# A hybrid decoder block: PSUM handed out by phases, score blocks taken two at a time, and another way to the sums of the MLP's entry

## The chip, the core and the metric

The kernel runs on one NeuronCore of a Trainium2 chip. Its time is the device time of one execution in microseconds (us). Five engines work side by side, each through its own queue in order: TensorE multiplies matrices (PE in the rows; PEld is its weight load), VectorE (DVE) and ScalarE (ACT) work on tiles, GpSimd (POOL) on tiles in SBUF, and SyncE (SP) issues transfers. TensorE writes into PSUM, which has eight banks of 512 fp32 values in each of 128 partitions; VectorE and ScalarE read it out.

## What is computed

The reference, cut to what matters (2048 tokens, width 1024, hidden width 4096, 16 query heads of 64 in 2 groups, window 128):

```python
hn = rmsnorm(x, norm_mix_g); proj = hn @ w_in          # LRU | gate | q | k | v
h = rg_lru(causal_depthwise_conv(x_lru), ...);  y_lru = h * gelu(g_lru)
scores = einsum(q, kwin) * scale                        # blocks of 128 queries, 2 key blocks
m = maximum(max(scores), sink); p = exp(scores - m)
probs = p / (sum(p) + exp(sink - m));  y_attn = einsum(probs, vwin)
x = x + concat(rmsnorm(y_lru), rmsnorm(y_attn)) @ w_out
hm = rmsnorm(x, norm_mlp_g)
x = x + square(relu(hm @ w_mlp_up)) @ w_mlp_down
return rmsnorm(x, norm_final_g)
```

## The kernel before

The tokens are taken in two chunks of 1024. Each chunk goes through input projection, attention, LRU, output projection and the up half of the MLP; the down half follows for both. Every matrix operand is split into a high part (made by ScalarE) and a low part (VectorE, `low = raw - high`), and a product is three matmuls: high by high, high by low, low by high.

**The order.** The program is written in Python as pieces of loops, and a list scheduler puts each engine's instructions into one fixed queue; the semaphore waits come from the tiles that an instruction reads or writes. A tile in PSUM has a tag, and a new tile of a tag waits until the readers of the last one are done. What is tracked is the tile, so two halves of one tile count as one.

**PSUM.** Two tiles of two banks each (tags mm0 and mm1) and four single banks (b01 twice, b2, b3) serve everything up to the end of the MLP's up half.

**Attention.** Heads come in turn (variable s, 16 passes a chunk). A pass has four steps p, and each step has: the scores of head s for two blocks (`scores`, 4 matmuls into a bank of tag b01, line L610), the products with the values of an older step (`values`, 24 short matmuls, L664), the transposes of the probabilities of head s - 1 (`probs`, two, L640, into one half of the bank tpb), and a piece of a projection (`piece`, 6 matmuls into a two-bank tile, L236 to L239; qps is the projection of a later pair of heads). VectorE puts the mask into the scores (L615 to L618), takes the maximum (L620, L621), and writes the low part of the transposed probabilities (pf, L644). When the projection of a pair of heads is complete (every second pass), ScalarE and VectorE read it out for one head and then for the other (L588 high, L589 low, named qs). A low weight tile wlo comes once for such a pair (L179).

**The MLP's up half.** It follows Strassen and Winograd: the normed activations hm are cut into quarters B11, B12, B21, B22, and their sums T1 = B12 - B11, T2 = B22 - T1, T3 = B22 - B12 and T4 = T2 - B21 are made once for a chunk, at its entry. Transposed blocks of the last token tiles arrive in PSUM (tps). VectorE takes T1 (L344) and T2 (L346) from them; ScalarE copies B12 into a tile x3 (L345), and VectorE subtracts it from B22 in PSUM to get T3 (L349). T1 overwrites B11 in the tile braw. The function `sums` then makes T4 (L365) and splits all into high (ScalarE, L360) and low (VectorE, L361). The low part of T2 is L350.

After that, 16 times a chunk, `pair(fp)` makes seven products of 12 matmuls (L410): A11 B11, A12 B21, S2 T2, A22 T4, S3 T3, S1 T1 and S4 B22, with weight sums S1 to S4 that GpSimd prepares (L388 to L391). pa and pb are single banks, and qr is a tile of two banks whose halves are pq (for A22 T4) and pr (for S1 T1, then S4 B22):

```python
qr = mm("qr", fp % 2)
pq, pr = qr[:, :HALF], qr[:, HALF:]
```

L440 reads pq on VectorE (`c2[:, lo] = pq + s3`); L443 reads pr after S1 T1, and L448 reads it after S4 B22. L453 to L456 combine the results. s12h and s12l are the high and low parts of S1 and S2, f2h and f2l those of S3 and A22, a1h and a1l those of A11 and A12.

The functions that the diff touches:

Of the kernel before, what the change touches and what calls it, by code (L numbers as in the profile page):

```python
# [37 lines left out]
def hybrid_block_kernel(  # L38
# [36 lines left out]
    def f32(ap):  # L75
        return ap.bitcast(F32)
# [5 lines left out]
    ps_stack = ExitStack()  # L82
    mmp = ps_stack.enter_context(tc.tile_pool(name="mmp", bufs=1, space=PSUM))
    hbp = ps_stack.enter_context(tc.tile_pool(name="hbp", bufs=1, space=PSUM))
# [26 lines left out]
    def bank(i, name, shape=(P, HALF)):  # L111
        if i < 2:
            return hbp.tile(list(shape), F32, name=name, tag="b01", bufs=2)
        return hbp.tile(list(shape), F32, name=name, tag=f"b{i}")
# [7 lines left out]
    def mm(name, i=None):  # L122

        if i is None:
            i = mm_next[0]
            mm_next[0] ^= 1
        return mmp.tile([P, D], F32, name=name, tag=f"mm{i}")

    def mm_halves(name, i=None):
        ps = mm(name, i)  # L130
        return [ps[:, :HALF], ps[:, HALF:]]
# [167 lines left out]
    class Up:  # L299
# [18 lines left out]
        def token_tile(self, t, src, g):  # L318
# [16 lines left out]
            if t == NT // 2 + 1:  # L335
                two = (P, 2, HALF)
                self.x3 = [U(q, "x3", F32, two) for q in range(2)]
                self.y2 = [U((2, 7)[q], "y2", F32, two) for q in range(2)]
                self.h["T2"] = self.quarter([H_TAG(0, p_, 2 + q) for p_ in range(2) for q in range(2)])
                self.h["B22"] = self.quarter([H_TAG(1, p_, 2 + q) for p_ in range(2) for q in range(2)])  # L340
            for q in range(2):
                o12, o22 = os[q], os[2 + q]
                t1, x3, y2 = self.braw[q][:, :, ts], self.x3[q][:, :, ts], self.y2[q][:, :, ts]
                dve.tensor_tensor(t1, o12, t1, op=ALU.subtract)  # L344
                act.activation(x3, o12, AF.Copy)  # L345
                dve.tensor_tensor(y2, o22, t1, op=ALU.subtract)  # L346
                hq = self.h["T2"]
                act.activation(hq[0][q][:, :, ts], y2, AF.Copy)
                dve.tensor_tensor(x3, o22, x3, op=ALU.subtract)  # L349
                dve.tensor_tensor(hq[1][q][:, :, ts], y2, f32(hq[0][q][:, :, ts]), op=ALU.subtract)  # L350
# [4 lines left out]
        def sums(self):  # L355
# [11 lines left out]
            split("T3", ("u6", "u3", "u5", "u4"), self.x3)  # L367
            split("T1", ("u8", "u9", "u2", "u7"), self.braw[:2])
# [48 lines left out]
        def pair(self, fp):  # L417

            pa, pb = bank(fp % 2 * 2, "pa"), bank(fp % 2 * 2 + 1, "pb")
            qr = mm("qr", fp % 2)  # L420
            pq, pr = qr[:, :HALF], qr[:, HALF:]
# [74 lines left out]
    def new_kv():  # L496
        k = mm("kps", 1)
        return k, ((k[:, :HALF], k[:, HALF:]), pair(0, "vps"))
# [11 lines left out]
    for c in range(NCH):  # L510
# [83 lines left out]
        class Head:  # L594
# [41 lines left out]
            def probs(self, p):  # L636

                tp = tpb[:, p % 2]
# [143 lines left out]
        for s in range(NH + 1):  # L782
            j = s // 2
            if s < NH:
                if s % 2 == 0:
                    yqs[j] = U(3 + j % 2, "yq", F32, (P, NT, P))
                heads[s] = Head(s, qs[j][s % 2], yqs[j])
# [5 lines left out]
            for p in range(4):  # L793
                if s < NH:
                    heads[s].scores(p)
                    if p == 3:
                        heads[s].sums()
# [3 lines left out]
                if s > 0:  # L801
                    heads[s - 1].probs(p)
                    late.append((s - 1, p))
                    if p == 3 and s % 2 == 1 and s > 1:
                        flip(j - 1, yqs[j - 1])
                piece(p if s % 2 else 4 + p)
# [118 lines left out]
        r_lr = token_rstd(accq, "lr")  # L925

# [166 lines left out]
    ps_stack.close()  # L1093
# [185 lines left out]
```

## Time and profile before

| | |
|---|---|
| median of 3 runs | 2512.08 us (2510.38 to 2513.5) |
| the profiled execution | 2512.32 us |
| its span, first to last instruction | 2510.6 us |
| TensorE busy | 2420.6 us (96% of the span) |
| VectorE busy | 1766.3 us (70%) |
| ScalarE busy | 1254.5 us (50%) |
| GpSimd busy | 457.4 us (18%) |
| mean granted TensorE clock | 0.996 of full speed |

The span is the profiled execution between its first and its last instruction, and its own time is 1.7 us more. Matmuls are pipelined, so one that lasts 0.39 us can be followed by the next after 0.23 us, and the busy time is that in which at least one is under way.

### The profile page before, as it was taken

Reading aid. Unit: us, or ns where it says so; the run is one execution under the profiler, and the core shown is the slowest. Engines: PE = TensorE matmul, PEld = TensorE weight load, DVE = VectorE, ACT = ScalarE, POOL = GpSimd, SP = SyncE. Lnnn points to the kernel's source line nnn. Section 1 sums busy time; section 2 is a strip of 40 time slices with the busy share of each in tenths; the row PEclk is TensorE's granted clock in tenths of the full one; section 3 lists DMA queues with packets and bytes.
Section 4 is the critical chain, followed back from the end, with each engine's and each line's share of the span. In section 5 each row is a group of like instructions: output and inputs, shape, how many; then the busy total and the mean of one; then the engine's idle time right before and its main releaser. Section 6 shows DMA issues by size and latency. Waiting matters only on the chain.

```text
span 2510.6 us, 32534 instructions
## 1 busy us (share of the span) xinstructions
PE 2420.6 (96%) x12338; PEld 1974.2 (79%) x12338; DVE 1766.3 (70%) x2400; ACT 1254.5 (50%) x2084; POOL 457.4 (18%) x455
## 2 busy tenths in 40 slices
PE   7999999999999998999999998999999999999998
PEld 6877787787788877887778787788878877888886
DVE  6887566756655565886667847655564898887889
ACT  6666777414455455666778315444554233322335
POOL 0445000001333210454000001322310110111100
PEclk9999999999999999999999999999999999999999
DMA  4111113312344443111113312344464454443334
GB/s 161 37 52 52 45 46 107 115 51 100 118 142 155 157 155 130 43 52 51 46 45 124 111 42 101 133 145 146 148 212 129 154 163 147 142 138 122 125 98 164
DMA packets 132812, 276.37 MB, mean 110 GB/s; under 512 B 11184, under 2 KB 70576, under 8 KB 132656
## 3 DMA queue, kind: packets, MB, share of 16 engines
q1 hardware_dynamic: 124880, 246.50, 29.4%
q0 software_dynamic: 5184, 18.88, 2.0%
q10 hardware_dynamic: 2592, 8.91, 0.9%
q8 instruction: 97, 1.59, 0.3%
q14 instruction: 59, 0.48, 0.1%
HBM read 190.37 MB, written 83.89 MB: 109 GB/s over the span
## 4 chain that ended last, share of the span: by engine, by line
PE 66%; DVE 15%; issue 9%; ACT 7%; DMA 2%; POOL 1%; POOLq 0%; SPq 0%; ACTq 0%; DVEq 0%
PE dd L1187 14%; PE ops L960 10%; PE qr L410 10%; PE pa L410 9%; PE pb L410 3%; PE sc L610 2%; PE qps L239 2%; PE qps L236 2%; PE qps L237 2%; DVE xc L719 2%; DVE acc L1196 1%; PE xps L237 1%; PE xps L236 1%; PE xps L239 1%; DVE wlo L179 1%
## 5 line engine op out<-in xcount | busy, mean ns | idle before, releaser
L1196 DVE TENSOR_TENSOR acc<-dd,acc 128x1024 f32<-128x1024 f32 x211 | 255.4, 1219 | 85.1 <-PE dd L1187 84.6
L960 PE MATMUL ops<-whi,ht 128*128 128x512 f32 x1024 | 278.4, 391 | 1.0 <-DVE x L965 1.0
L990 ACT ACTIVATE ah<-araw 128x1024 fp32r<-128x1024 f32 x96 | 101.9, 1062 | 293.0 <-PE dd L1187 286.6
L960 PEld LDWEIGHTS ops<-whi,ht 128*128 128x128 f32 x1024 | 192.2, 188 | 42.7 <-DVE x L965 2.5
L960 PE MATMUL ops<-wlo,ht 128*128 128x512 f32 x512 | 159.7, 391 | 0.6 <-DVE wlo L179 0.5
L388 POOL TENSOR_TENSOR s<-wraw 128x512 f32<-128x512 f32 x32 | 43.0, 1343 | 593.2 <-issue 321.0
L178 ACT ACTIVATE whi<-wraw 128x1024 fp32r<-128x1024 f32 x84 | 88.5, 1054 | 120.7 <-PE ops L960 86.2
L647 POOL TENSOR_SCALAR_AFFINE_SELECT pf<-pf 128x512 f16<-128x512 f16 x128 | 87.3, 682 | 333.4 <-DVE pf L644 327.0
L991 DVE TENSOR_TENSOR al<-araw,ah 128x1024 fp32r<-128x1024 f32 x96 | 123.4, 1287 | 11.0 <-ACT ah L990 10.9
L624 ACT ACTIVATE st<-sc,mx 128x128 f32<-128x128 f32 x256 | 91.6, 364 | 60.1 <-DVE mx L621 59.6
L179 DVE TENSOR_TENSOR wlo<-wraw,whi 128x1024 fp32r<-128x1024 f32 x84 | 106.5, 1274 | 20.0 <-ACT whi L178 9.5
L960 PEld LDWEIGHTS ops<-wlo,ht 128*128 128x128 f32 x512 | 95.5, 188 | 21.4 <-DVE wlo L179 2.3
L236 PE MATMUL qps<-ht,whi 128*128 128x512 f32 x256 | 107.8, 421 | 0.0
L396 ACT ACTIVATE f2h<-wraw 128x1024 fp32r<-128x1024 f32 x32 | 33.9, 1061 | 142.6 <-DMA act<-hid 111.9
L237 PE MATMUL qps<-ht,whi 128*128 128x512 f32 x256 | 101.7, 397 | 0.0
L236 PE MATMUL xps<-ht,whi 128*128 128x512 f32 x256 | 101.5, 397 | 0.0
L239 PE MATMUL qps<-ht,wlo 128*128 128x512 f32 x256 | 101.3, 396 | 0.0
L237 PE MATMUL xps<-ht,whi 128*128 128x512 f32 x256 | 101.0, 394 | 0.0
L236 PE MATMUL gpps<-ht,whi 128*128 128x512 f32 x256 | 100.8, 394 | 0.0
L410 PE MATMUL qr<-hm,s 128*128 128x512 f32 x384 | 97.6, 403 | 2.7 <-DVE hid L443 2.7
L237 PE MATMUL gpps<-ht,whi 128*128 128x512 f32 x256 | 100.1, 391 | 0.0
L397 DVE TENSOR_TENSOR f2l<-wraw,f2h 128x1024 fp32r<-128x1024 f32 x32 | 39.1, 1223 | 79.1 <-ACT f2h L396 79.1
(327 smaller groups left out, 6852.5 us busy)
## 6 DMA issues: line engine op xcount, KB each, us to landing
araw<-act SPq DMA_DIRECT2D x96, 512.0 KB, 3.5
wraw<-in_w_up_dram SPq DMA_DIRECT2D x64, 512.0 KB, 3.2
act<-hid SPq DMA_DIRECT2D x128, 256.0 KB, 2.6
wraw<-in_w_in_dram SPq DMA_DIRECT2D x52, 512.0 KB, 3.2
act<-a SPq DMA_DIRECT2D x96, 256.0 KB, 2.6
wraw<-in_w_out_dram SPq DMA_DIRECT2D x32, 512.0 KB, 3.2
braw<-in_w_down_dram SPq DMA_DIRECT2D x28, 512.0 KB, 4.3
xt<-in_x_dram SPq DMA_DIRECT2D x16, 512.0 KB, 4.6
```

The lines of the kernel that those rows point to most:

```text
L178: act.activation(hi, raw, AF.Copy)
L179: (eng or dve).tensor_tensor(lo, raw, f32(hi), op=ALU.subtract)
L236: pe.matmul(ps[m], w[0][:, k * P:(k + 1) * P], hk(ht[m][0], k), start=(k == 0), stop=False)
L237: pe.matmul(ps[m], w[0][:, k * P:(k + 1) * P], hk(ht[m][1], k), start=False, stop=False)
L239: pe.matmul(ps[m], w[1][:, k * P:(k + 1) * P], hk(ht[m][0], k), start=False, stop=(k == KT - 1))
L410: pe.matmul(ps, w[a_][:, ks], hk(h[b_], k), start=first and k == 0 and i == 0, stop=k == KT // 2 - 1 and i == 2, skip_group_check=True)
L624: ins = act.activation(self.st[:, b, :], cur[:, i, :], AF.Exp, bias=self.mx[:, b:b + 1], accum_out=self.ls[:, b:b + 1])
L960: pe.matmul(ps[m], a_, wk[k][b_][:, hs], start=(k == 0 and a_ is yh and b_ == 0), stop=(k == kn - 1 and a_ is ylo))
L990: act.activation(hi, raw, AF.Copy)
L991: dve.tensor_tensor(lo, raw, f32(hi), op=ALU.subtract)
L1187: pe.matmul(o[:, i, :], a_[:, t0:t0 + P], b_[:, r, :], start=first and r == 0 and k == 0, stop=r == 1 and k == 2, skip_group_check=True)
L1196: dve.tensor_tensor(accs[blk][d_], o, accs[blk][d_], op=ALU.add)
```

## The change

It has three parts.

First, PSUM is opened anew for each phase. A function `psum` closes the pools of the last phase and opens the next. In the phases "sbp" (the start, the output projection and the MLP's up half) there are eight single banks s0 to s7; in the phase "doubles" (from the keys and values to the end of the LRU) there are the two double tiles and four single banks as before. In the MLP pq and pr thereby become two tiles, and what was qr is gone.

Second, attention takes the steps p two at a time: two score blocks, then the older values, then two sets of transposes, then two pieces. The transposes of odd steps no longer go to tpb, but to halves of the double tile that no projection uses at the time (`free`); even steps keep a half of tpb each.

Third, at the MLP's entry T1 gets a tile of its own (t1) and no longer overwrites B11 in braw. The copy x3 and its subtraction from PSUM are gone; T3 is made in `sums` as T2 - B11 from tiles in SBUF (`t3 = y2 - braw`, which is B22 - B12 again), in one subtraction of 1024 columns for each of the two q.

```diff
     slots = ctx.enter_context(tc.tile_pool(name="slots", bufs=1))
-    ps_stack = ExitStack()
-    mmp = ps_stack.enter_context(tc.tile_pool(name="mmp", bufs=1, space=PSUM))
-    hbp = ps_stack.enter_context(tc.tile_pool(name="hbp", bufs=1, space=PSUM))
+    phase = [None, {}]
+    def psum(*names):
+        if phase[0]:
+            phase[0].close()
+        phase[:] = [ExitStack(), {}]
+        for name in names:
+            phase[1][name] = phase[0].enter_context(
+                tc.tile_pool(name=name, bufs=1, space=PSUM, reuse_waits="tile"))
+    def doubles():
+        psum("mmp", "hbp")
+    psum("sbp")
...
     def bank(i, name, shape=(P, HALF)):
+        if "sbp" in phase[1]:
+            return half(4 + i, name)
         if i < 2:
-            return hbp.tile(list(shape), F32, name=name, tag="b01", bufs=2)
-        return hbp.tile(list(shape), F32, name=name, tag=f"b{i}")
+            return phase[1]["hbp"].tile(list(shape), F32, name=name, tag="b01", bufs=2)
+        return phase[1]["hbp"].tile(list(shape), F32, name=name, tag=f"b{i}")
+    def half(i, name):
+        return phase[1]["sbp"].tile([P, HALF], F32, name=name, tag=f"s{i}")
...
             mm_next[0] ^= 1
-        return mmp.tile([P, D], F32, name=name, tag=f"mm{i}")
+        return phase[1]["mmp"].tile([P, D], F32, name=name, tag=f"mm{i}")
     def mm_halves(name, i=None):
+        if "sbp" in phase[1]:
+            if i is None:
+                i = mm_next[0]
+                mm_next[0] ^= 1
+            return [half(2 * i, name), half(2 * i + 1, name)]
         ps = mm(name, i)
...
                 two = (P, 2, HALF)
-                self.x3 = [U(q, "x3", F32, two) for q in range(2)]
+                self.t1 = [U(q, "t1", F32, two) for q in range(2)]
                 self.y2 = [U((2, 7)[q], "y2", F32, two) for q in range(2)]
                 self.h["T2"] = self.quarter([H_TAG(0, p_, 2 + q) for p_ in range(2) for q in range(2)])
                 self.h["B22"] = self.quarter([H_TAG(1, p_, 2 + q) for p_ in range(2) for q in range(2)])
             for q in range(2):
                 o12, o22 = os[q], os[2 + q]
-                t1, x3, y2 = self.braw[q][:, :, ts], self.x3[q][:, :, ts], self.y2[q][:, :, ts]
-                dve.tensor_tensor(t1, o12, t1, op=ALU.subtract)
-                act.activation(x3, o12, AF.Copy)
+                t1, y2 = self.t1[q][:, :, ts], self.y2[q][:, :, ts]
+                dve.tensor_tensor(t1, o12, self.braw[q][:, :, ts], op=ALU.subtract)
                 dve.tensor_tensor(y2, o22, t1, op=ALU.subtract)
-                hq = self.h["T2"]
-                act.activation(hq[0][q][:, :, ts], y2, AF.Copy)
-                dve.tensor_tensor(x3, o22, x3, op=ALU.subtract)
-                dve.tensor_tensor(hq[1][q][:, :, ts], y2, f32(hq[0][q][:, :, ts]), op=ALU.subtract)
+                act.activation(self.h["T2"][0][q][:, :, ts], y2, AF.Copy)
+            hq = self.h["T2"]
+            for q in range(2):
+                dve.tensor_tensor(hq[1][q][:, :, ts], self.y2[q][:, :, ts], f32(hq[0][q][:, :, ts]),
+                                  op=ALU.subtract)
             hq = self.h["B22"]
...
             split("T4", ("u16", "u17", "u18", "u19"), t4)
-            split("T3", ("u6", "u3", "u5", "u4"), self.x3)
-            split("T1", ("u8", "u9", "u2", "u7"), self.braw[:2])
+            t3 = self.braw[:2]
+            for q in range(2):
+                dve.tensor_tensor(t3[q], self.y2[q], t3[q], op=ALU.subtract)
+            split("T3", ("u6", "u3", "u5", "u4"), t3)
+            split("T1", ("u8", "u9", "u2", "u7"), self.t1)
...
             pa, pb = bank(fp % 2 * 2, "pa"), bank(fp % 2 * 2 + 1, "pb")
-            qr = mm("qr", fp % 2)
-            pq, pr = qr[:, :HALF], qr[:, HALF:]
+            pq, pr = half(fp % 2 * 2, "pq"), half(fp % 2 * 2 + 1, "pr")
             lo, hi = slice(0, HALF), slice(HALF, D)
...
     def new_kv():
+        doubles()
         k = mm("kps", 1)
...
-            def probs(self, p):
-                tp = tpb[:, p % 2]
+            def probs(self, p, free):
+                if p % 2 and free:
+                    tp = free[p // 2][:, :2 * P].rearrange("p (a n) -> p a n", a=2)
+                else:
+                    tp = tpb[:, p // 2]
                 for i in range(2):
...
             j = s // 2
+            free = mm_halves("tp", (s + 1) // 2 % 2) if 0 < s < NH - 1 else None
             if s < NH:
...
                     piece, done = (new_x if j + 2 == KT else new_gate)(0)
-            for p in range(4):
+            for p0 in (0, 2):
                 if s < NH:
-                    heads[s].scores(p)
-                    if p == 3:
+                    for p in (p0, p0 + 1):
+                        heads[s].scores(p)
+                    if p0:
                         heads[s].sums()
                 if len(late) == 4:
                     for _ in range(2):
                         heads[late[0][0]].values(late.pop(0)[1])
                 if s > 0:
-                    heads[s - 1].probs(p)
-                    late.append((s - 1, p))
-                    if p == 3 and s % 2 == 1 and s > 1:
+                    for p in (p0, p0 + 1):
+                        heads[s - 1].probs(p, free)
+                        late.append((s - 1, p))
+                    if p0 and s % 2 == 1 and s > 1:
                         flip(j - 1, yqs[j - 1])
-                piece(p if s % 2 else 4 + p)
+                for p in (p0, p0 + 1):
+                    piece(p if s % 2 else 4 + p)
             if s % 2 == 0:
...
         r_lr = token_rstd(accq, "lr")
+        psum("sbp")
...
     up.run(ahead)
-    ps_stack.close()
+    phase[0].close()
     ddp = ctx.enter_context(tc.tile_pool(name="ddp", bufs=4, space=PSUM, reuse_waits="tile"))
```

Lines of the new kernel are about 22 to 35 higher: L589 is L614, L640 is L668, L644 is L672, L664 is L692, L410 is L435, L440 is L464, L443 is L467, L365 is L387, L361 is L383. T3's subtraction is L391.

What moves in the queues. On VectorE in attention, this stands in a queue of a steady pair of heads from the weight tile wlo to the first pf after the projection's read-out (qs); before:

```order
L179 TENSOR_TENSOR wlo<-wraw,whi 128x1024 [waits DMAHW0_49,PE_49]
L632 TENSOR_TENSOR ls<-ls,es 128x8 [waits Activation_49]
L615 COPY_PREDICATED sc<-prevm,negt 128x128 [waits PE_49]
L633 TENSOR_SCALAR ls<-ls 128x8 [waits DVE_49]
L616 COPY_PREDICATED sc<-prevm,sc 128x128 [waits DVE_49]
L634 RECIPROCAL ls<-ls 128x8 [waits DVE_49]
L620 TENSOR_REDUCE mx<-sc 128x2 [waits DVE_49]
L589 SCALAR_TENSOR_TENSOR qs<-qps,qs 64x1024 [waits Activation_49]
L621 TENSOR_SCALAR mx<-mx,snk 128x2 [waits DVE_49]
L644 SCALAR_TENSOR_TENSOR pf<-tp,pf 128x256 [waits Activation_49]
```

and now:

```order
L201 TENSOR_TENSOR wlo<-wraw,whi 128x1024 [waits DMAHW1_49,PE_49]
L640 COPY_PREDICATED sc<-prevm,negt 128x128 [waits PE_49]
L614 SCALAR_TENSOR_TENSOR qs<-qps,qs 64x1024 [waits Activation_49]
L641 COPY_PREDICATED sc<-prevm,sc 128x128 [waits DVE_49]
L643 COPY_PREDICATED sc<-prevm,sc 128x2x128 [waits PE_49]
L645 TENSOR_REDUCE mx<-sc 128x2 [waits DVE_49] x2
L614 SCALAR_TENSOR_TENSOR qs<-qps,qs 64x1024 [waits Activation_49]
L646 TENSOR_SCALAR mx<-mx,snk 128x2 [waits DVE_49] x2
L672 SCALAR_TENSOR_TENSOR pf<-tp,pf 128x256 [waits PE_49,Pool_49]
```

The small row sums ls (L632 to L634) stand ahead of wlo now; both score blocks of the double step (three copies and two maxima) stand between the first qs and the second.

On TensorE the same pair of heads has two groups of 12 projection matmuls in a pass in place of four groups of 6. Over both chunks, places where transposes into tp are followed by another kind of work go from 116 to 100, and for all transposes from 167 to 149. The first transposes of an odd step into the free tile, in the pass that follows the read-out, stand behind the scores of a double step, 24 values, two transposes, 12 projection matmuls and 8 more values, and wait for VectorE and TensorE.

On TensorE in the MLP, this stands where S1 T1 begins (s12h) in a steady pair; before:

```order
L410 MATMUL pa<-hm,a1l 128x512
L410 MATMUL pb<-hm,a1h 128x512
L410 MATMUL qr<-hm,s12h 128x512 [waits DVE_49]
L410 MATMUL qr<-hm,s12h 128x512
L410 MATMUL qr<-hm,s12l 128x512
```

and now:

```order
L435 MATMUL pa<-hm,f2h 128x512 x2
L435 MATMUL pa<-hm,f2l 128x512
L435 MATMUL pr<-hm,s12h 128x512 x2
L435 MATMUL pr<-hm,s12l 128x512
L435 MATMUL pr<-hm,s12h 128x512 x2
```

S1 T1 stands behind S3 T3 (f2h, f2l into pa) and has no wait for VectorE any more; before, it stood behind A11 B11 and the first matmul of A12 B21 of the next pair. S4 B22 keeps its wait for VectorE (L467), with four matmuls of the next pair ahead of it.

On VectorE at the first chunk's entry into the MLP, for the last token tile (y is T2, t is T1, hm the split parts of all sums); before:

```order
L344 TENSOR_TENSOR braw<-tps,braw 128x2x256 [waits PE_49]
L344 TENSOR_TENSOR braw<-tps,braw 128x2x256 [waits Activation_49]
L346 TENSOR_TENSOR y_5816<-tps,braw 128x2x256 [waits DVE_49,PE_49]
L349 TENSOR_TENSOR x_5814<-tps,x_5814 128x2x256
L346 TENSOR_TENSOR y_5817<-tps,braw 128x2x256 [waits DVE_49]
L349 TENSOR_TENSOR x_5815<-tps,x_5815 128x2x256 [waits Activation_49]
L350 TENSOR_TENSOR hm<-y_5816,hm 128x2x256 [waits Activation_49]
L350 TENSOR_TENSOR hm<-y_5817,hm 128x2x256 [waits Activation_49]
L365 TENSOR_TENSOR braw<-braw,y_5816 128x1024
L224 TENSOR_TENSOR hm<-tps,hm 128x2x256 [waits Activation_49]
L365 TENSOR_TENSOR braw<-braw,y_5817 128x1024
```

and now:

```order
L366 TENSOR_TENSOR t_5865<-tps,braw 128x2x256 [waits PE_49]
L366 TENSOR_TENSOR t_5866<-tps,braw 128x2x256 [waits PE_49]
L367 TENSOR_TENSOR y_5867<-tps,t_5865 128x2x256 [waits DVE_49,PE_49]
L367 TENSOR_TENSOR y_5868<-tps,t_5866 128x2x256 [waits DVE_49,PE_49]
L387 TENSOR_TENSOR braw<-braw,y_5867 128x1024 [waits DVE_49]
L371 TENSOR_TENSOR hm<-y_5867,hm 128x2x256 [waits Activation_49]
L371 TENSOR_TENSOR hm<-y_5868,hm 128x2x256 [waits Activation_49]
L246 TENSOR_TENSOR hm<-tps,hm 128x2x256 [waits Activation_49] x2
L387 TENSOR_TENSOR braw<-braw,y_5868 128x1024
L383 TENSOR_TENSOR hm<-braw,hm 128x1024 [waits Activation_49]
L391 TENSOR_TENSOR braw<-y_5867,braw 128x1024
```

The two x rows and ScalarE's copies in front of them are gone, T1 and T2 follow one another, the first T4 subtraction stands ahead of T2's low part, and the T3 subtraction (L391, two in all) stands between the low parts of T4. Up to the low part a1l, the queue has 20 rows from the first T1 row before and 18 now. On TensorE 75 MLP matmuls stand ahead of the first that needs a1l, where 66 stood; and ScalarE's s12h for the second pair now waits for the last matmul of the first pair's S1 T1, which stands right ahead of the second pair's S2 T2.

## Rows read from the trace of the kernel before

**Rows 1.** The page, part 1: busy time, share of the span, instructions.
```profile
PE 2420.6 (96%) x12338; PEld 1974.2 (79%) x12338; DVE 1766.3 (70%) x2400; ACT 1254.5 (50%) x2084; POOL 457.4 (18%) x455
```

**Rows 2.** TensorE's waits: total us, times, longest.
```profile
PE tp L640 <- DVE pf L644: 13.2, 16, 1.1
...
PE pa L410 <- ACT hm L348: 7.1, 2, 3.5
...
PE qr L410 <- DVE hid L440: 5.5, 4, 4.2
```

**Rows 3.** Busy time by stretch, attention and MLP: us, PE, PEld, DVE.
```profile
50.00:250.00 200.00, 190.54 (x1675) 159.72 (x1675) 161.26 (x417) 124.17 (x398) 91.41 (x135) 1.00 0.13 46
650.00:930.00 280.00, 279.38 (x1208) 224.21 (x1207) 155.43 (x175) 139.18 (x165) 82.40 (x56) 1.00 0.43 147
```

**Rows 4.** Timeline of TensorE in attention: start, us, what.
```profile
118.16 0.44 PE L640 MATMUL tp<-ident,st 128*128 128x128 f32 x2 [0.83 <-DVE pf L644]
...
125.33 0.40 PE L610 MATMUL sc<-kcar,qs 128*128 128x256 f32 x2
...
125.80 0.87 PE L664 MATMUL av<-vpa,pf 128*128 128x64 f16 x24
126.51 0.42 PE L640 MATMUL tp<-ident,st 128*128 128x128 f32 x2
126.69 0.48 PE L236 MATMUL qps<-ht,whi 128*128 128x512 f32 x1
127.00 0.40 PE L237 MATMUL qps<-ht,whi 128*128 128x512 f32 x1
```

**Rows 5.** Timeline of VectorE in attention, same pair of heads.
```profile
113.14 1.63 DVE L179 TENSOR_TENSOR wlo<-wraw,whi 128x1024 fp32r<-128x1024 f32 x1
...
116.30 1.22 DVE L589 SCALAR_TENSOR_TENSOR qs<-qps,qs 64x1024 fp32r<-64x1024 f32 x1
...
117.69 0.42 DVE L644 SCALAR_TENSOR_TENSOR pf<-tp,pf 128x256 f16<-128x256 f32 x1
...
118.93 1.23 DVE L589 SCALAR_TENSOR_TENSOR qs<-qps,qs 64x1024 fp32r<-64x1024 f32 x1
```

**Rows 6.** Timeline of TensorE in one steady MLP pair.
```profile
783.92 0.39 PE L410 MATMUL pb<-hm,a1h 128*128 128x512 f32 x1
784.20 0.73 PE L410 MATMUL qr<-hm,s12h 128*128 128x512 f32 x2
784.77 0.39 PE L410 MATMUL qr<-hm,s12l 128*128 128x512 f32 x1
...
787.05 0.39 PE L410 MATMUL pb<-hm,a1h 128*128 128x512 f32 x1
```

**Rows 7.** Timeline of VectorE in the same pair.
```profile
783.46 0.68 DVE L440 TENSOR_TENSOR hid<-qr,s 128x512 f32<-128x512 f32 x1
```

**Rows 8.** Timeline of VectorE at the first chunk's MLP entry.
```profile
627.58 0.69 DVE L344 TENSOR_TENSOR braw<-tps,braw 128x512 f32<-128x512 f32 x1 [0.66 <-ACT x L345]
...
633.52 1.71 DVE L365 TENSOR_TENSOR braw<-braw,y 128x1024 f32<-128x1024 f32 x1
...
644.76 1.21 DVE L378 TENSOR_TENSOR a1l<-wraw,a1h 128x1024 fp32r<-128x1024 f32 x1
```

**Rows 9.** Timeline of TensorE at that entry.
```profile
630.50 0.51 PE L410 MATMUL pa<-hm,s12h 128*128 128x512 f32 x1 [3.54 <-ACT hm L348]
...
646.03 0.50 PE L410 MATMUL pa<-hm,a1l 128*128 128x512 f32 x1
```

**Rows 10.** Timeline of GpSimd at that entry.
```profile
634.23 2.17 POOL L389 TENSOR_TENSOR s<-s,wraw 128x512 f32<-128x512 f32 x1
```

**Rows 11.** Timeline of TensorE at the second chunk's MLP end.
```profile
1870.24 1.19 PE L410 MATMUL qr<-hm,s12h 128*128 128x512 f32 x2 [4.18 <-DVE hid L440]
...
1875.64 3.06 PE L410 MATMUL qr<-hm,s 128*128 128x512 f32 x12 [0.79 <-DVE hid L443]
```

**Rows 12.** Timeline of VectorE there.
```profile
1869.51 0.68 DVE L440 TENSOR_TENSOR hid<-qr,s 128x512 f32<-128x512 f32 x1
```

## Prediction

> **What bounds the kernel now.** I read the page's busy times first: TensorE is busy 2420.6 us of a span of 2510.6, so at most 90 us can be had without taking matmuls away, and the change takes none away [rows 1]. The waits of TensorE come second, since only what ends one of them counts: the longest sum is 13.2 us in 16 waits of transposes in attention for VectorE's pf, then 7.1 us at the two MLP entries and 5.5 us of S1 T1 for L440, of which one wait alone is 4.2 [rows 2]. The windows come third: TensorE leaves 9.5 of 200 us idle in attention, where VectorE is busy 161 of 200, and 0.6 of 280 in the steady MLP, where VectorE is busy 155 [rows 3]. So VectorE, in order and four fifths full, sets attention's pace at the moments when TensorE needs it, while in the MLP little more than the beat of the matmuls is to be had. Then I followed each place in the timelines.
>
> **Attention.** Once in a pair of heads the second transposes wait 0.83 us, until 118.16 [rows 4]. The cause is VectorE's queue: the weight tile wlo starts at 113.14, the first read-out qs at 116.30 takes 1.22, and only then comes the pf (117.69, 0.42) that has to leave the bank which both transposes share [rows 5]. After the change that wait goes, since odd steps have a tile of their own. But that tile is the one from which qs was read, so the first odd transposes now wait for the second qs read-out. In the old order this ends at 118.93 + 1.23 = 120.16, 7.0 us after wlo's start [rows 5].
>
> I walk the new order from wlo's start (0). VectorE: wlo 1.2 to 1.6 (1.63 at 113.14 [rows 5]), one short mask copy, the first qs to about 2.9, then copies and two maxima, about 1.5 (an estimate from the 0.42 of pf, which is of the same 256 columns), the second qs from 4.2 to 5.4. TensorE, from the projection's last matmul, which I take to fall on the same moment, since the first read-out waits for it: two groups of scores at 0.47 each (125.33 to 125.80), 24 values 0.71 (to 126.51), two transposes 0.18 (to 126.69), and 12 projection matmuls, 0.31 for the first and 0.23 for each of the others [rows 4, 6], 2.8 in all, then 8 values 0.24: the odd transposes are reached at 4.9. The new wait is 0.5 (0.3 to 0.8 with wlo's two durations). The next, even, transposes wait for a pf that stands right behind the second qs, ready at 6.1, when TensorE comes at 5.9 to 6.1: 0 to 0.35. I take 0.65 for a pair; bounds 0.3 and 1.15. For 16 such waits that is 10.4 in place of 13.2: **-2.8** (-8.4 to +5).
>
> A matmul behind transposes starts 0.31 after the one before it, not 0.23 [rows 4, 6]; 18 such places fewer at 0.08 give **-1.4**. The scores, values and transposes themselves stay the same in number.
>
> **The steady MLP.** In a pair S1 T1 starts at 784.20, 0.28 after the matmul before it, where 0.23 is the beat (787.05 - 784.77 over 10 matmuls), and its third matmul follows after 0.57 in place of 0.46: 0.05 + 0.11, so 0.17 lost [rows 6]. It waits for L440, which begins at 783.46, takes 0.68 and reads pq, the other half of the same tile [rows 7]. With two tiles this wait is gone from the order. About 30 of the 32 pairs are steady: **-5.1**. The bound on the other side is 0: S4 B22 still waits for VectorE (L467), now with S1 T1 earlier, and L464 and L467 may stand in one another's way there.
>
> **The MLP's entries.** VectorE is the bound from the last token tile's transposes to a1l: its first T1 waits 0.66 us at 627.58 for ScalarE's copy, and a1l ends at 644.76 + 1.21 = 645.97 [rows 8]; TensorE waits 3.54 for T2 until 630.50, and the first matmul with a1l comes at 646.03 [rows 9]. Out go two subtractions of 512 columns at 0.69 on VectorE and the wait of 0.66; one row of 512 columns for the hidden sum moves behind a1l, 0.69 again; in come two subtractions of 1024 columns at 1.21: 2.7 less and 2.4 more, so a1l ends within 0.3 of where it did. T2's high part no longer stands behind two copies on ScalarE and comes 0.5 to 1 earlier. What counts then is that 75 matmuls stand ahead of the first with a1l, not 66: 9 x 0.23 = 2.0, and with the 0.5 at the start 2.5. Against it stands s12h for the second pair, which now waits for the last S1 T1 of the first, right ahead of that pair's S2 T2: a read-out of 1.1 to 1.2 us (I take a ScalarE tile of 1024 columns to last as VectorE's 1.21 [rows 8]) that nothing covers. **-1.3** for a chunk, **-2.6** for both; bounds -6 and 0.
>
> The same subtraction L365 took 1.71 us at 633.52, while GpSimd was at 634.23 in an addition of weights [rows 8, 10], and 1.21 is what a1l of the same size takes without GpSimd. So the two new subtractions can cost 0.5 more each where they meet GpSimd, 1.0 for a chunk. The Trainium skill (SBUF — State Buffer, Who interferes with whom) says that a VectorE instruction with two inputs in SBUF and a GpSimd instruction that reads SBUF shut each other out of a shared port, while one with a single SBUF input does not; by that rule the change trades two subtractions that GpSimd can't delay for two that it can, which speaks against it. The longer row agrees in its direction, and by the rule the entries would give -0.6 in place of -2.6.
>
> **The end of the second chunk's MLP.** S1 T1 waits 4.18 us until 1870.24 [rows 11] for L440, which VectorE reaches only at 1869.51, behind tiles of the down half [rows 12]. It does not need L440's result, only the release of pq's half. Afterwards it can run in that gap, at once behind S3 T3, and S4 B22 waits for L467 instead. It started at 1875.64 [rows 11]. L467 still stands in the same queue behind the same down-half tiles, and by that queue ends near 1872.4 to 1873.9. So **-2.5** (-1.7 to -3.2). The same mechanism is smaller at the first chunk's end, where the transposes of the next chunk fill in; I count nothing there, with 2 to either side.
>
> **The sum.** -2.8 - 1.4 - 5.1 - 2.6 - 2.5 = -14.4 from the profiled execution's 2512.3, whose span is 2510.6 and which lies 0.2 above the median of the three runs: about 2498. A measurement of this kernel tells 0.2% (5 us) from no change.
>
> **Rivals.**
> - *The second qs is late (slower).* If VectorE stays as far behind as in the old order, where that read-out ends 7.0 after wlo, the odd transposes wait 2.0 us for a pair, not 0.83: 16 x 1.2 = +19, and with the other terms (-11.6) +7: 2519. For it: VectorE is 81% busy, and whatever delays its queue by 1 us hits TensorE at once, for the two transposes in the shared tile have no cover. Against it: the two qs come closer together in the new order, without the row sums and the pf that stood between. It outweighs the rest once the wait exceeds about 1.6 us in each pair.
> - *Gains given back at the next wait (no change).* Attention at its bad bound (+5 - 1.4), S4 B22 taking over the 0.17 in each steady pair, the entries at 0, and only the tail's -2.5: +1: 2513. For it: in each place the instruction behind the removed wait waits for the same engine. Against it: in the steady MLP VectorE is busy only 155 of 280 us [rows 3].
> - *The new wait in attention is at its short bound (faster still).* -8.4 - 1.4 - 5.1 - 4 - 3.2 = -22: 2490. It needs VectorE to finish the second qs before 4.9.
> - *The entry does nothing.* VectorE's queue there is as long as before. Then the sum is -12 and the case is still the main one, at 2500.
>
> **The numbers.** The main case 0.58 (2492 to 2505, 2498 the likeliest), the short bound 0.12, given back 0.18, the late qs 0.12. The range leaves out the latter's upper part and the lower half of the third: 2487 to 2515. Faster by over 0.2%: 0.58 + 0.12 = 0.70; within: 0.18; slower: 0.12.
>
> **What would show it.** In attention the wait of transposes for pf (13.2) shrinks, and one for the qs read-out comes up, under 0.8 us each; over 1.6 makes me wrong. In the steady MLP the first of S1 T1's matmuls follows at the beat, and a pair takes 0.17 less; if S4 B22's wait grows by as much, that term is 0. At the entry TensorE meets T2 before 630 and a1l about where it did. At the second chunk's end no wait above 2 us stands before S1 T1, and the first matmul of the down half comes 1.7 to 3.2 sooner.

## The result and the profile after

The changed kernel takes 2569.7 us (2564.96 to 2572.04), the kernel before 2511.2 beside it: a ratio of 1.023 (1.0211 to 1.025). It is 58 us slower where I forecast 14 faster. From the page of the changed kernel (span, then busy time, share of the span and instructions):

```profile
span 2570.3 us, 32626 instructions
...
PE 2433.8 (95%) x12338; PEld 1991.5 (77%) x12338; DVE 1741.4 (68%) x2396; ACT 1251.3 (49%) x2076; POOL 447.7 (17%) x455
```

It has the same 12338 matmuls, and no engine has more instructions than before [rows 1]. VectorE, ScalarE and GpSimd are a little less busy. TensorE is busy 13.2 us longer with the same matmuls; the mean granted clock fell from 0.996 to 0.979 of full speed, and I put the 13.2 down to that. So of the 59.7 us that the span grew, 46.5 are waiting and 13.2 slower matmuls, and nothing is new work. TensorE's waits after the change (total us, times, longest):

```profile
PE sqt L729 <- POOL accq L935: 44.2, 2, 22.6
...
PE tp L668 <- DVE qs L614: 8.3, 6, 2.5
PE pr L435 <- DVE hid L467: 7.7, 4, 2.2
...
PE tp L668 <- DVE pf L672: 1.4, 3, 0.8
```

The wait of the attention transposes for pf (13.2 before [rows 2]) is nearly gone, and one for the read-out qs stands in its place, as foretold. But 44.2 us go by in two waits that the prediction does not name: sqt, the transposes for the LRU's row sums, wait for GpSimd's last addition into accq, once a chunk. Before the change it is

```profile
PE sqt L701 <- POOL accq L901: 2.7, 2, 1.7
```

so these two waits alone grew by 41.5 us. TensorE at the first of them, in the kernel before:

```profile
459.27 1.09 PE L701 MATMUL sqt<-ident,accq 128*128 128x128 f32 x8 [0.99 <-POOL accq L901]
```

and in the changed one:

```profile
444.05 0.39 PE L915 MATMUL gps<-xhi,gd 128*128 128x512 f32 x1
467.00 1.97 PE L729 MATMUL sqt<-ident,accq 128*128 128x128 f32 x8 [22.56 <-POOL accq L935]
468.62 1.20 PE L995 MATMUL ops<-whi,ht 128*128 128x512 f32 x2
```

Between the LRU's last gate matmuls (gps) and sqt lies the chain of the LRU's last columns: sigmoids, table loads and exponentials on ScalarE, products and a scan on VectorE, the square, and GpSimd's addition. That chain is little shorter in the kernel before: from the last gps matmul to sqt it takes 21.3 us in both chunks there, and 23.0 and 22.3 now. GpSimd's addition alone takes 2.36 and 2.35 us before, 3.69 and 3.49 now. What filled the chain is seen in the windows (us, then busy time and instructions of PE, PEld, DVE, ACT, POOL; PEclk; DMA share and GB/s) of the 23 us ahead of sqt, first in the kernel before:

```profile
436.00:459.00 23.00, 21.95 (x95) 17.33 (x93) 20.32 (x24) 18.79 (x25) 3.75 (x4) 1.00 0.57 196
```

and then in the changed one, in the first chunk, the 13 us behind that gap, and in the second chunk:

```profile
444.00:467.00 23.00, 0.44 (x3) 0.01 (x2) 17.31 (x18) 17.25 (x22) 5.29 (x4) 0.54 0.57 202
467.00:480.00 13.00, 13.00 (x55) 11.02 (x56) 5.82 (x10) 0.37 (x2) 1.12 (x2) 0.89 0.32 110
1403.00:1426.00 23.00, 1.34 (x6) 0.80 (x5) 15.72 (x17) 16.33 (x20) 5.65 (x5) 0.50 0.57 204
```

89 of the 95 matmuls there are of the output projection (ops), on the attention half of its input, which needs nothing of the LRU; the others are the last gps. Now there are 3 or 6 in all, gps and sqt, and no ops. In and right after the gap TensorE has the lower of its two clock levels (0.5 of full speed, 1.2 GHz): the two matmuls at 468.62 take 1.20 us together, and the granted clock of the 13 us from 467 is 0.89.

The order of TensorE's queue says the same: before the change 110 output-projection matmuls of a chunk stand ahead of sqt, 26 of them even ahead of the last gps; after the change none does. `psum("sbp")` stands in the program behind `r_lr = token_rstd(accq, "lr")` and ahead of the loop of the output projection. It closes the pools of which sqt's tiles are the last and opens the one from which every ops tile comes; and in the queue all ops now stand behind all of the old phase's matmuls.

The start times of some instructions in the traces show where it goes; each figure is the changed kernel's start less that of the kernel before, in us, and what is added between two rows is lost there:

| first start of | chunk 0 | chunk 1 |
|---|---|---|
| first scores | +3.4 | +38.3 |
| sqt for accq | +7.7 | +35.2 |
| last matmul of the output projection | +31.7 | +61.6 |
| last matmul of the MLP's up half (S4 B22) | +29.6 | +59.4 |

So 24.0 and 26.4 us are lost in the two output projections, 3.4 at the start, and 8.7 from the first chunk's MLP to the second's scores (38.3 less 29.6). The attention and LRU stretches give +4.3 and -3.1, the MLPs -2.1 and -2.2. The 3.4 at the start, which every run with the phases shows (2.8 to 4.1), I did not trace.

The 8.7 has the same form. TensorE after the first chunk's last product:

```profile
984.56 0.41 PE L240 MATMUL tps<-ident,xt 128*128 128x128 f32 x2 [2.27 <-DVE xt L230]
...
986.92 2.82 PE L240 MATMUL tps<-ident,xt 128*128 128x128 f32 x12 [0.65 <-DVE xt L230]
992.86 0.80 PE L258 MATMUL kps<-ht,whi 128*128 128x512 f32 x1 [3.12 <-DVE ht L246]
```

`new_kv` opens the double phase, and kps is its first tile. It stands behind all transposes (tps) of the next chunk's input, of the old phase; before, 16 of them stood among the kps matmuls, which covered their waits. Behind these waits the clock is low here too:

```profile
992.00:1003.00 11.00, 10.14 (x32) 8.12 (x33) 1.94 (x3) 1.06 (x1) 0.00 (x0) 0.68 0.71 239
```

At a granted clock of 0.68 these 11 us are about 3.5 lost (an estimate, 0.32 x 11), so a good part of the 8.7 is the clock and not the waits.

### The profile page after: what moved, and what is told of

Same layout as the page of the kernel before. It is cut to its first block, busy times and chain, and to the rows that moved or that the text cites. A ratio compares the mean times of both kernels' runs of the same rounds, so it can differ in the third digit from the quotient of the medians.

```text
span 2570.3 us, 32626 instructions
## 1 busy us (share of the span) xinstructions
PE 2433.8 (95%) x12338; PEld 1991.5 (77%) x12338; DVE 1741.4 (68%) x2396; ACT 1251.3 (49%) x2076; POOL 447.7 (17%) x455
## 4 chain that ended last, share of the span: by engine, by line
PE 66%; DVE 16%; issue 8%; ACT 7%; POOL 1%; DMA 1%; POOLq 0%; SPq 0%; ACTq 0%; DVEq 0%
PE dd L1222 14%; PE ops L995 13%; PE pa L435 9%; PE pr L435 7%; PE pq L435 3%; PE pb L435 3%; DVE xc L747 2%; PE sc L635 1%; DVE acc L1231 1%; PE xps L259 1%; PE xps L258 1%; PE xps L261 1%; DVE wlo L201 1%; DVE qs L614 1%; DVE r L926 1%
## 5 line engine op out<-in xcount | busy, mean ns | idle before, releaser
L675 POOL TENSOR_SCALAR_AFFINE_SELECT pf<-pf 128x512 f16<-128x512 f16 x128 | 96.2, 751 | 336.7 <-DVE pf L672 329.1
L1000 DVE SCALAR_TENSOR_TENSOR x<-ops,rs_at,x 128x512 f32<-128x512 f32 x96 | 67.6, 745 | 61.6 <-PE ops L995 56.1
L435 PE MATMUL pr<-hm,s 128*128 128x512 f32 x384 | 101.3, 415 | 7.7 <-DVE hid L467 7.7
```

Of the source, the lines that this page charges most:

```text
L435: pe.matmul(ps, w[a_][:, ks], hk(h[b_], k), start=first and k == 0 and i == 0, stop=k == KT // 2 - 1 and i == 2, skip_group_check=True)
L675: nc.gpsimd.affine_select(out=pf[:, 1], in_=pf[:, 0], compare_op=ALU.is_gt, fill=0.0, base=0, pattern=[[0, 4], [-1, P]], channel_multiplier=1)
```

## The experiments

I took the theory that the switch between pools is what costs (A), and against it that the new work in attention or at the entry makes the gaps (B).

**Keeping the double phase.** The changed kernel without the switch at the output projection and without a second opening of the same phase; pq and pr are halves of one tile again:

```diff
         r_lr = token_rstd(accq, "lr")
-        psum("sbp")
...
     def new_kv():
-        doubles()
+        if "mmp" not in phase[1]:
+            doubles()
...
-            pq, pr = half(fp % 2 * 2, "pq"), half(fp % 2 * 2 + 1, "pr")
+            qr = mm("qr", fp % 2)
+            pq, pr = qr[:, :HALF], qr[:, HALF:]
```

> The changed kernel, but PSUM stays in the double-tile phase from the first keys and values to the end of the MLP's up half: no switch ahead of the output projection, none back at the second chunk, and so pq and pr are halves of one tile again. Attention's double steps and the entry's new sums stay. Theory A: the switch of pools puts the 110 output-projection matmuls of a chunk that stood ahead of sqt behind it, and kps of the second chunk behind all tps, and that is the loss; then about 24 + 26 + 9 us come back: 2512 (2508 to 2518). Rival B: the loss comes from attention's double steps or the entry, whose queues feed the places where the trace shows the gaps; then it stays above 2555.

Measured: 2517.2 us, ratio 1.0018 (1.0009 to 1.0027). 53 of the 58 us are back, with attention's and the entry's changes still in, and the wait of sqt is small again:

```profile
PE sqt L731 <- POOL accq L937: 3.0, 2, 1.7
```

Its start is 3.6 late at the first scores, since the switch there is still in, and nothing is lost at the second chunk's start (+7.2 at the last product, +7.2 at the first kps).

**The phases alone**, on the kernel before, with the old attention and entry (the parts of the diff in `probs`, the pass loop and the entry left out).

> The kernel before with the phases of PSUM alone (with pq and pr as two tiles in the MLP, which come with them); attention and the entry are as before. Theory A: the whole loss is here, 2567 to 2576. Rival B: about 2511, less up to 5 for pq and pr.

Measured: 2572.2 us, ratio 1.0234 (1.0221 to 1.0247). The whole loss is here, and the long wait of sqt with it:

```profile
PE sqt L723 <- POOL accq L925: 44.7, 2, 22.6
```

B falls.

**The switch one statement earlier:**

```diff
                 tp = bank(2 + hf, "sqt", (P, 4, P))
+                if "sbp" in phase[1]:
+                    tp = tp.rearrange("p (a n) -> p a n", a=4)
...
+        psum("sbp")
         r_lr = token_rstd(accq, "lr")
-        psum("sbp")
```

The first two added lines only give the tiles of sqt, which now come from the new phase, the shape that they had.

> The changed kernel with the switch to eight single banks one statement earlier, ahead of the row sums of the LRU (sqt) in place of behind them. In TensorE's queue 75 of the 110 matmuls then stand ahead of sqt, none ahead of the last gate matmuls gps. Theory A (order in TensorE's queue): 75 x 0.23 = 17 us of each of the two 22 us gaps are filled, and less time goes by at half clock: 2528 to 2538. Rival A2 (the gap is a wait of the new tiles for the old tiles' readers, wherever the switch stands): no change, 2565 to 2573.

Measured: 2528.8 us, ratio 1.0066 (1.0053 to 1.0079). sqt after it:

```profile
465.27 1.60 PE L731 MATMUL sqt<-ident,accq 128*128 128x128 f32 x8 [4.17 <-POOL accq L937]
```

The wait of 22.56 is 4.17, with 75 of 110 matmuls ahead of sqt. Only the place of one statement moved, and 41 us came back: the tiles of the output projection are eight single banks as in the changed kernel, so neither they nor a wait for the old tiles' readers made the 22 us gap, but the order in the queue. The 35 matmuls that still stand behind sqt are 8 us at 0.23, and from sqt to the last matmul of the output projection 7.3 and 9.2 us are lost in the two chunks.

**The switch at the last part of the output projection**, where no work of the new phase could run ahead of the old one's last:

```diff
         r_lr = token_rstd(accq, "lr")
-        psum("sbp")
...
                 if last:
+                    psum("sbp")
                     g2 = load_g(g_mlp)
```

> The changed kernel with the switch to eight single banks moved from the start of the output projection to its last part (four of its 16 weight rows are left then), where the tiles of the new phase have no work that could run ahead of the old phase's last. 110 output-projection matmuls stand ahead of sqt in TensorE's queue again, as before the change. Theory A: both 22 us gaps go, and what is left over the kernel before are the switches at the start and at the second chunk (3 and 9) and the entry (2 a chunk), less attention (3) and the steady pairs and tails (8): 2512 to 2522. Rival (a switch costs its 20 us wherever it stands): 2550 or more.

Measured: 2523.1 us, ratio 1.0044 (1.0029 to 1.0058); a little above the range that I gave, and far from 2550. All 110 matmuls are ahead of sqt. What a switch costs is mostly what stands on its two sides. By itself it costs something too: the first matmul of the new phase waits for VectorE to read out the last tiles of the old one,

```profile
574.62 0.73 PE L995 MATMUL ops<-whi,ht 128*128 128x512 f32 x2 [2.42 <-DVE x L1000]
```

and 2.37 us in the second chunk, waits that the kernel before does not have there. From sqt to the last output-projection matmul 2.3 us are lost in one chunk and 3.9 in the other (+5.8 to +8.1 and +10.4 to +14.3), so these waits are all of it in the one and over half in the other.

**Attention's double steps alone**, on the kernel before.

> The kernel before with attention's double steps alone (odd transposes in the free double tile), no phases, old entry. My prediction's step: 4 us faster, 2507. What the milestones of the changed kernel's trace say: attention 3.1 longer in the first chunk, 3.3 shorter in the second: 2511 (2508 to 2514).

Measured: 2508.3 us, ratio 0.9986 (0.9977 to 0.9994): 3.5 us faster, close to my step's 4.2, and more than the starts in the changed kernel's trace had made me expect.

**pq and pr as two tiles alone**, without phases:

```diff
-            qr = mm("qr", fp % 2)
-            pq, pr = qr[:, :HALF], qr[:, HALF:]
+            pq, pr = mm("pq", 0)[:, :HALF], mm("pr", 1)[:, :HALF]
```

> The kernel before with pq and pr of the MLP as two tiles alone: pq takes a half of one double tile, pr a half of the other, for every pair; no phases. My prediction's step: S1 T1 no longer waits for L440, 0.17 in each of 30 pairs, and the gap at the second chunk's end shrinks by 2.5: 2503 to 2505. Rival: the next wait (S4 B22 for L443) takes it all: 2509 to 2512.

Measured: 2504.9 us, ratio 0.9975 (0.9966 to 0.9984), 6.3 faster. TensorE in a steady pair of this kernel:

```profile
778.94 0.39 PE L410 MATMUL pa<-hm,f2l 128*128 128x512 f32 x1
779.16 0.61 PE L410 MATMUL pr<-hm,s12h 128*128 128x512 f32 x2
779.62 0.39 PE L410 MATMUL pr<-hm,s12l 128*128 128x512 f32 x1
...
782.83 3.06 PE L410 MATMUL pr<-hm,s 128*128 128x512 f32 x12
```

S1 T1 follows after 0.22 and its third matmul after 0.46, where it was 0.28 and 0.57 [rows 6], and S4 B22 (782.83) does not wait.

**The entry's new sums alone**, on the kernel before.

> The kernel before with the entry's new sums alone (T1 in its own tile, T3 from SBUF), no phases, one tile for pq and pr. My prediction's step: 2.6 faster for both chunks, 2508.5 (2506 to 2511). Rival, by the longer subtractions beside GpSimd: no change, 2510 to 2512.5.

Measured: 2515.5 us, ratio 1.0012 (1.0003 to 1.0021): 3 us slower, outside both. TensorE there:

```profile
638.63 0.80 PE L413 MATMUL pa<-hm,f2h 128*128 128x512 f32 x1 [1.89 <-ACT hm L360]
640.95 0.79 PE L413 MATMUL pa<-hm,f2h 128*128 128x512 f32 x1 [1.52 <-DVE hm L361]
```

and VectorE, ScalarE and GpSimd:

```profile
635.18 3.44 DVE L369 TENSOR_TENSOR braw<-y,braw 128x1024 f32<-128x1024 f32 x2
...
637.52 2.19 ACT L360 ACTIVATE hm<-braw 128x1024 fp32r<-128x1024 f32 x2 [3.83 <-DVE braw L369]
...
634.13 2.27 POOL L393 TENSOR_TENSOR wraw<-wraw 128x512 f32<-128x512 f32 x1
```

S3 T3 (f2h into pa) waits for the high part of T3, which ScalarE can only begin at 637.52, when VectorE has made T3 behind T4. Before the change ScalarE made T3's high parts ahead of T4's, between 630.85 and 633.3, from a T3 that came straight out of PSUM. T2 is there sooner, as foretold (TensorE waits 2.58 us for it, where it waited 3.54 [rows 9]); with the waits for T3 the waits of this stretch grow from 6.5 us to 7.0 in all. a1l starts at 643.09 in place of 644.76 [rows 8], but the whole entry starts 2.7 us earlier in this run (the last 14 transposes of the token tiles start at 622.52, not 625.21); counted from there it is 1.0 later. Nothing waited for it. Behind the waits for T3 the clock is low, where it was 1.00 in the same 4 us before:

```profile
641.00:645.00 4.00, 4.00 (x10) 3.19 (x11) 3.90 (x4) 0.00 (x0) 0.48 (x1) 0.53 0.00 0
```

That alone is about 1.9 us (an estimate, 0.47 x 4).

**The entry with T3 ahead of T4** (the two blocks in `sums` exchanged).

> The kernel before with the entry's new sums alone, as in the run of the entry, but the T3 subtraction and its split ahead of T4's. Theory: the entry lost because T3 is made behind T4 and its subtractions run beside GpSimd, so that S3 T3 waits; with T3 first the wait goes over to A22 T4, which is needed a product earlier, and nothing is won: 2513 to 2518. Rival: only T3's place was wrong, then A22 T4 is still in time and the entry is as short as before or shorter: 2508 to 2512.

Measured: 2516.2 us, ratio 1.0016 (1.0007 to 1.0025). The loss stays, and the wait has gone over to A22 T4, as expected:

```profile
642.50 0.79 PE L413 MATMUL qr<-hm,f2h 128*128 128x512 f32 x1 [1.81 <-DVE hm L361]
```

So it is not T3's place among the sums that is at fault. That it is the chain of VectorE work, which got two longer links, is argued from the two orders and not shown by itself.

**pq and pr with the entry**, and **everything but the phases.**

> Both of these on the kernel before: two tiles for pq and pr, and the entry's new sums, without phases and with the old attention. If the steps add: 2500 to 2503. If one hides the other: that of the split alone.

> Everything of the change but the phases: attention's double steps, the entry's new sums, and pq and pr as halves of two different double tiles, all in the pools of before. Theory A says that this is the gain that I predicted with the switches taken out: 2498 to 2505. If attention's double steps give nothing, it equals the split with the entry.

Measured: 2509.7 us, ratio 0.9992 (0.9983 to 1.0001), and 2506.7 us, ratio 0.9982 (0.9973 to 0.9991). Both miss their expectations, which still had the entry as a gain. From the last output-projection matmul to the fifth pair it takes 86.3 and 86.6 us in the two chunks before, 87.6 and 89.3 with the split alone, 88.9 and 88.1 with the entry alone, and 91.8 and 90.8 with both. So the split pays for its gains at the entry as well. In the second chunk the two add (2.7 and 1.5 make 4.2), in the first they cost 1.6 more together than apart. Whether the steps add in the times can't be told: the split with the entry should give -3.3 and gives -2.0, everything but the phases should give -6.8 and gives -4.5, and each of these times is known to about 2.3.

**pq and pr with attention's double steps**, the old entry, no phases.

> The kernel before with two of the change's three gains: attention's double steps, and pq and pr as halves of two different double tiles; no phases, and the old sums at the MLP's entry. Alone the one gave 3.6 us and the other 6.3. If they add: 2501 to 2504, faster than every kernel so far. If the output projection or the second chunk's start gives one of them back: 2504 to 2508.

Measured: 2504.1 us, ratio 0.9966 (0.9954 to 0.9979): 8.5 us faster than before, the lowest time of all kernels here, though not told apart from that of the split alone; within the noise the two gains add (3.5 and 6.3).

## Why the prediction was wrong, step by step

**The step that failed is one that is missing.** The sum counts what the phases give in the MLP, and puts the switches themselves at nothing without a word: the start and the output projection don't occur in it, and of the first chunk's end it looks only at the wait of S1 T1 ("I count nothing there, with 2 to either side"). What it leaves out is that a switch puts the new phase's matmuls behind all of the old one's, so that they no longer cover a wait that stands between. The phases alone are +60 (2572.2 against 2512.6). Taken apart by the starts in that kernel's trace: the start +4.1 at the first scores, the output projections +25.4 and +25.9 (from +5.4 to +30.8, from +40.3 to +66.2), the second chunk's start +8.5 (+30.8 to +39.2), the second MLP -6.5 (+66.2 to +59.7), and 2.3 in attention and the LRU of both chunks. The parts leave little room for anything else: phases +60, attention -3.5 and the entry +3 make +59, and the changed kernel measured +58, each time known to a few us.

What would have told it was at hand: in the trace before, 23 us of LRU latency ahead of sqt, filled by 89 output-projection matmuls, and in the changed kernel's queue the same matmuls behind sqt. The list of what moves in the queues names attention, the MLP and its entry, and not this place. A wait of 1 us stood there (2.7 in both chunks), short enough to be passed over. The price of a lost cover is not the wait that is there, but the work that stands in front of it.

**Attention: -4.2 predicted, -3.5 measured.** The mechanism was as described, its size differently spread. In the first chunk the odd transposes wait for qs, five times 1.17 us and once 2.46:

```profile
193.86 0.41 PE L668 MATMUL tp<-ident,st 128*128 128x128 f32 x2 [1.17 <-DVE qs L614]
```

VectorE there, from wlo to the second qs:

```profile
188.07 1.17 DVE L201 TENSOR_TENSOR wlo<-wraw,whi 128x1024 fp32r<-128x1024 f32 x1
189.16 0.73 DVE L640 COPY_PREDICATED sc<-prevm,negt 128x128 f32<-128x128 uint32 x1
189.92 1.22 DVE L614 SCALAR_TENSOR_TENSOR qs<-qps,qs 64x1024 fp32r<-64x1024 f32 x1
...
192.49 1.23 DVE L614 SCALAR_TENSOR_TENSOR qs<-qps,qs 64x1024 fp32r<-64x1024 f32 x1
```

From wlo's start the second qs ends at 5.65 (I had 5.4), but TensorE is there at 4.6, not 4.9, since wlo started 0.46 after the projection's end and not with it: 1.17 where I took 0.5, just above the upper bound of 1.15 for a pair. In the second chunk, where one mask copy for both blocks stands in place of L640 and L641, no wait of transposes for qs shows at all. In the run of attention alone the first chunk loses 2.7 us from the first scores to sqt, and the second gains 4.2: -1.4 in all. (In the changed kernel the longer chain ahead of sqt adds 1.6 and 1.0, which makes the +4.3 and -3.1 above.) The rest of the measured -3.5 (whose interval is -5.8 to -1.5) lies in small pieces behind attention, 0.8 of it in the first output projection and 1.1 in the second MLP, and I did not trace it.

**The steady MLP: -5.1 predicted.** The 11 periods from A11 of the fifth to A11 of the sixteenth pair take 213.75 us before and 211.59 in the changed kernel in each chunk: 0.20 a period, where I had 0.17. There are fewer steady pairs than the 30 that I counted: the first four of a chunk are of the entry and keep other periods. For about 12 a chunk it is -4.7. S4 B22's wait did not take it over: it shows in the first pairs and the last one, not in the steady ones.

**The end of the second chunk's MLP: -2.5 predicted.** It was right in kind, mis-sized in the split alone: from the sixteenth pair to the last product it takes 26.0 us, not 31.8, so -5.8, and in the changed kernel 27.7, so -4.1. S4 B22 waits 2.16 for L467 there, and S1 T1's gap of 4.18 [rows 11] is gone:

```profile
1933.50 4.61 PE L435 MATMUL pr<-hm,s 128*128 128x512 f32 x12 [2.16 <-DVE hid L467]
```

These 12 matmuls take 4.61 us here and 3.06 in the steady pair above; the granted clock from 1934.2 to 1937.6 is 0.51, and that is most of the difference between -5.8 and -4.1. At the first chunk's end, where I counted nothing, the split alone brings the last product 8.5 us nearer to the sixteenth pair, but the second chunk's first scores only 0.4, so nothing was about right.

**The entries: -2.6 predicted, +3 measured.** The sign was wrong. I summed VectorE's queue up to a1l; the product that TensorE reached first was S3 T3, whose operand had become later by two subtractions and a split, and I had not walked that chain. The 1.21 us taken for the new subtractions was wrong too: two of them took 3.44 beside GpSimd in the run of the entry alone, 1.0 more than I took, and a1l came 1.0 later where I had it within 0.3. In the changed kernel one took 2.31:

```profile
666.36 2.31 DVE L391 TENSOR_TENSOR braw<-y,braw 128x1024 f32<-128x1024 f32 x1
...
670.81 1.21 DVE L391 TENSOR_TENSOR braw<-y,braw 128x1024 f32<-128x1024 f32 x1
```

The first ran beside two subtractions of GpSimd (665.43 for 2.15 us, 667.55 for 2.25), the second beside none. The Trainium skill (SBUF — State Buffer, Who interferes with whom) says that a VectorE instruction with two inputs in SBUF contends with a GpSimd instruction that reads SBUF; that the slower of two like instructions is 1.1 us longer agrees in its direction with that rule. Which share of the 3 us is this, which the longer chain and which the low clock behind its waits was not separated. In the changed kernel the stretch from the last output-projection matmul to the fifth pair is 2.3 and 4.1 us longer than before, but the phases alone make it 4.1 and 1.6 longer, so the entry's part in it can't be read there.

**The rivals.** The late qs did come, but in one chunk only, and of its six waits one was above 1.6 us. The short bound, no wait for qs, came in the other chunk. "Gains given back at the next wait" came at the entry, where more was given back than gained, and not in the steady MLP. "The entry does nothing" was too kind. None of them is the loss of 58 us.

## What to carry to other kernels

Where memory is handed out by phases and a scheduler sets the order, look first at what crosses each boundary in the old queue: count the instructions that stood ahead of the old phase's last one and came from the new one, and multiply by their beat. 110 matmuls at 0.23 are 25 us, which is what each output projection lost. A short wait behind a long latency chain can mean that something covers it; name the cover before you move anything. A dependency between two halves of a tile can be lifted by giving each a half of another tile that is there already, with no boundary at all.

## What was not expected of the hardware

After a gap of 22.56 us TensorE's first matmuls went at half of full speed (the two at 468.62 took 1.20 us, where two take 0.62 a few us later). At this one place the clock is small beside the gap: 0.89 over 13 us is about 1.4 us lost (an estimate, 0.11 x 13). Over the whole kernel it is not: TensorE was busy 13.2 us longer with the same matmuls, over a fifth of the 59.7, and the clock was low behind much shorter waits too, as at the second chunk's start (0.68 over 11 us behind one of 3.12). An fp32 subtraction of 1024 columns on VectorE, 1.21 us alone, took up to 2.31 beside GpSimd's subtractions.
